# Streaming the high and low parts of the moving tokens as one operand of 512 columns in a two-block transformer kernel

## The chip, the core and the metric

The kernel runs on one core of a Trainium2 chip. The time is the device time of one execution in microseconds (us), median of several runs. TensorE (PE) does the matmuls, with a second row, PEld, for its weight loads; VectorE (DVE), ScalarE (ACT) and GpSimd (POOL) work beside it; SyncE (SP) issues most DMAs.

## The reference, cut to what matters

Two transformer blocks run on 256 tokens of width 1024, all in float32. Cut to the parts that the change touches:

```python
# block 1
x = x + merged @ w_out                                # merged: attention and pooling, gated
h2 = rmsnorm(x, norm_mlp_g)
z = square(relu(h2 @ w_up))                           # "FFN1", width 4096
x = x + z @ w_down
x = rmsnorm(x, final_norm_g)
# block 2
x = x + mix @ w_out_2                                 # mix: sparse attention and linear attention, gated
mem_n = rms_norm(mem, ln_mem_g)                       # 256 memory rows
q = rms_norm(x, ln_x_g) @ w_xq * 128 ** -0.5          # "cross attention", 4 heads of 128
k, v = split(mem_n @ w_xkv, 2)
x = x + (softmax(q @ k.T) @ v) @ w_xo
u, g = split(rms_norm(x, ln_ffn_g) @ w_up_2, 2)       # "FFN2", width 2816
u = conv_w[0] * u[t-2] + conv_w[1] * u[t-1] + conv_w[2] * u[t] + conv_b
x = x + (gelu(u) * g) @ w_down_2
return rms_norm(x, ln_final_g)
```

## The kernel before

Every large matrix product is made exact enough by splitting both sides into a high and a low part (`split`: ACT copies the high part, DVE subtracts to get the low part) and summing three matmuls: high by high, high by low and low by high (`mm3`, lines 196 to 198). Weights come in chunks of 512 KB by DMAs from SP into four `raw` buffers; ACT writes `whi` (line 158), DVE writes `wlo` (line 159), seven buffers each. Both engines run in order, so an eviction can stand behind a weight split of 1.0 to 1.2 us.

There are two forms of product. In `linB` and in the down projections (`mm_out`, `last_rows`) a block of 128 tokens is the stationary operand and 512 columns of a weight matrix move. In `linA` (and in `first_pair`, which does the same for the first two column blocks of an FFN while the tokens are still being made) a 128 x 128 piece of the weights is stationary and all 256 tokens move; the result is transposed, as the next product needs it. `linA` covers 256 output columns in two halves m = 0, 1, each of eight k steps of one `mm3`: 48 matmuls of 256 columns. Both halves lie in one PSUM bank `mm`; after both, one eviction per `linA` follows. The pools `mm` and `tp` have two banks each, `ph` four. The activations are kept as separate high and low tiles (`actah`, `actal`, `actbh`, `actbl`, and `memh`, `meml` for the memory).

FFN1 has 16 column blocks. For block b the order is `linA` of block b + 2, then 24 matmuls of 512 columns that add block b's share of the down projection into the four `ph` banks. The eviction (`relu2`) is one DVE step, max(ps, 0) times the token's scale r (the rms factor, spread over partitions as the row tile `rbc`), then the square, the copy to `zh` on ACT, and the subtraction to `zl` on DVE. FFN2 has 11 blocks; for each, two `linA` (u, then g) are followed by the 24 matmuls. Its eviction `ev_u` multiplies by the scale row, does the convolution and the gelu, and POOL multiplies by the scale row again; `ev_g` multiplies by g straight from PSUM. Cross attention uses `linA` for keys (of the memory) and queries.

`rows_bc` (lines 259 to 269) makes the scale row: POOL makes two diagonal matrices `diag` (line 265), two matmuls with a matrix of ones put them into a `tp` bank (line 266), ACT copies it out. It runs once in each FFN, between the two halves of `first_pair`, and once in the cross attention.

Each `after` step at the end of a block's last down projection transposes the new x (line 243, `tp`), multiplies by the gain and splits it. At the very end a loop over the two token blocks adds the last down projection to x (line 360), squares (ACT), multiplies by the gain (line 1356), sums (line 1359), takes the power on POOL (line 1360), scales half on ACT (line 1361) and half on DVE (line 1363), and stores each half by a DMA.

## Time and profile before

| | |
|---|---|
| runs | 832.72, 831.82, 832.34 us; median 832.34 us |
| profiled execution | 831.34 us, of which the span 829.6 us |
| TensorE busy | 809.7 us, 98% of the span |
| DVE, ACT, POOL busy | 532.9 us (64%), 441.7 us (53%), 90.5 us (11%) |
| granted TensorE clock, mean | 0.998 of full speed |
| DMA | 142 MB, mean 171 GB/s |

The span is what the profiler saw between the first and the last instruction; the execution's own time is 1.7 us longer. A row of a matmul group gives the time from a matmul's start to its modelled end, and consecutive matmuls overlap: the time that one takes from the next is read from the distance of starts, called the pitch below.

### The profile page before, as it was taken

To read this page: it belongs to the slowest core of one execution; us is meant where nothing else is said; L and a number is where in the kernel's file an instruction comes from. 1 tells how busy PE (TensorE), PEld (TensorE's weight loads), DVE (VectorE), ACT (ScalarE), POOL (GpSimd) and SP (SyncE) were. 2 spreads that over 40 slices of the span, in tenths; PEclk is the share of its full clock that TensorE was granted. 3 is DMA by queue.
4 is the path that set the end of the run, shared out by engine and by line. 5 is a ranking of instruction groups with operands and counts; after the bars stand their busy time and mean duration, and the time that the engine had idled before them with its cause. 6 is when DMAs were issued, how large, how long until landed. Compare 5 with 4: busy or idle time off the path is not lost.

```text
span 829.6 us, 12764 instructions
## 1 busy us (share of the span) xinstructions
PE 809.7 (98%) x4875; PEld 698.0 (84%) x4875; DVE 532.9 (64%) x872; ACT 441.7 (53%) x715; POOL 90.5 (11%) x144
## 2 busy tenths in 40 slices
PE   6999999999999999999999999999999999999996
PEld 5877878888999999988867778888988999999995
DVE  6757687667655555567588564579556866666563
ACT  5636565536554544556466455466554745545442
POOL 4500500102000000015000010000202100100001
PEclk9999999999999999999999999999999999999999
DMA  8854546654665565578523427672551765656621
GB/s 276 276 179 129 149 128 177 206 151 147 210 201 180 185 195 186 176 248 253 164 77 103 130 76 206 198 226 98 194 169 45 227 215 178 195 171 191 198 82 51
DMA packets 86732, 142.01 MB, mean 171 GB/s; under 512 B 5951, under 2 KB 50755, under 8 KB 86672
## 3 DMA queue, kind: packets, MB, share of 16 engines
q1 hardware_dynamic: 84976, 138.07, 54.3%
q0 software_dynamic: 1104, 1.92, 0.9%
q10 hardware_dynamic: 592, 1.22, 0.4%
q8 instruction: 38, 0.62, 0.3%
q14 instruction: 22, 0.18, 0.1%
HBM read 140.14 MB, written 1.05 MB: 170 GB/s over the span
## 4 chain that ended last, share of the span: by engine, by line
PE 90%; DVE 3%; DMA 2%; ACT 2%; POOL 1%; issue 1%; SPq 0%; POOLq 0%; ACTq 0%
PE mm L196 18%; PE mm L198 17%; PE mm L197 17%; PE ph L356 6%; PE ph L353 6%; PE ph L352 6%; PE ph L196 3%; PE ph L198 3%; PE ph L197 3%; PE tp L243 1%; DMA raw<-in_w_in 1%; DVE wlo L159 1%; PE ph L938 1%; DMA x<-in_x 1%; ACT whi L158 1%; PE ph L987 1%
## 5 line engine op out<-in xcount | busy, mean ns | idle before, releaser
L159 DVE TENSOR_TENSOR wlo<-raw,whi 128x1024 fp32r<-128x1024 f32 (+1 forms) x254 | 310.5, 1227 | 204.1 <-ACT whi L158 201.3
L158 ACT ACTIVATE whi<-raw 128x1024 fp32r<-128x1024 f32 (+1 forms) x254 | 264.9, 1051 | 229.0 <-PE mm L197 80.1
L196 PE MATMUL mm<-actbh,whi 128*128 128x256 f32 x368 | 104.1, 283 | 0.5 <-ACT actbh L158 0.5
L197 PE MATMUL mm<-actbl,whi 128*128 128x256 f32 x368 | 104.1, 283 | 0.0
L198 PE MATMUL mm<-actbh,wlo 128*128 128x256 f32 x368 | 104.1, 283 | 0.0
L353 PE MATMUL ph<-wlo,zh 128*128 128x512 f32 x188 | 73.6, 391 | 0.0
L352 PE MATMUL ph<-whi,zh 128*128 128x512 f32 x188 | 73.5, 391 | 0.0
L196 PEld LDWEIGHTS mm<-actbh,whi 128*128 128x128 f32 x368 | 69.9, 190 | 1.3 <-ACT actbh L158 1.0
L197 PEld LDWEIGHTS mm<-actbl,whi 128*128 128x128 f32 x368 | 70.0, 190 | 0.4
L198 PEld LDWEIGHTS mm<-actbh,wlo 128*128 128x128 f32 x368 | 70.0, 190 | 0.0
L196 PE MATMUL mm<-actah,whi 128*128 128x256 f32 x240 | 67.9, 284 | 0.5 <-ACT actah L158 0.5
L197 PE MATMUL mm<-actal,whi 128*128 128x256 f32 x240 | 68.0, 283 | 0.0
L198 PE MATMUL mm<-actah,wlo 128*128 128x256 f32 x240 | 67.9, 283 | 0.0
L196 PE MATMUL mm<-whi,actbh 128*128 128x512 f32 (+1 forms) x168 | 65.2, 389 | 0.1
L197 PE MATMUL mm<-wlo,actbh 128*128 128x512 f32 (+1 forms) x168 | 65.1, 388 | 0.0
L198 PE MATMUL mm<-whi,actbl 128*128 128x512 f32 (+1 forms) x168 | 64.9, 386 | 0.0
L198 PE MATMUL mm<-whi,actal 128*128 128x512 f32 x160 | 64.9, 405 | 0.0
L197 PE MATMUL mm<-wlo,actah 128*128 128x512 f32 x160 | 64.6, 404 | 0.0
L196 PE MATMUL mm<-whi,actah 128*128 128x512 f32 x160 | 64.6, 405 | 0.0
L356 PE MATMUL ph<-whi,zl 128*128 128x512 f32 x188 | 58.4, 392 | 0.0
L196 PEld LDWEIGHTS mm<-actah,whi 128*128 128x128 f32 x240 | 45.6, 190 | 1.5 <-ACT actah L158 1.0
L197 PEld LDWEIGHTS mm<-actal,whi 128*128 128x128 f32 x240 | 45.7, 190 | 0.5
(423 smaller groups left out, 1482.5 us busy)
## 6 DMA issues: line engine op xcount, KB each, us to landing
raw<-in_w_in SPq DMA_DIRECT2D x79, 512.0 KB, 4.1
raw<-in_w_up SPq DMA_DIRECT2D x76, 512.0 KB, 4.0
raw<-in_w_down SPq DMA_DIRECT2D x54, 512.0 KB, 4.3
raw<-in_w_out SPq DMA_DIRECT2D x16, 512.0 KB, 3.5
raw<-in_w_xkv SPq DMA_DIRECT2D x8, 512.0 KB, 3.9
raw<-in_w_branch_nsa SPq DMA_DIRECT2D x8, 256.0 KB, 4.3
raw<-in_w_branch_gla SPq DMA_DIRECT2D x4, 512.0 KB, 3.7
raw<-in_w_xq SPq DMA_DIRECT2D x4, 512.0 KB, 3.5
```

Of the source, the lines that this page charges most:

```text
L158: ia = A.activation(hi, src, AF.Copy)
L159: iv = sub.tensor_tensor(lo, src, hi.bitcast(F32), op=OP.subtract)
L196: PE.matmul(ps, sh, mh, start=start, stop=False)
L197: PE.matmul(ps, sh, ml, start=False, stop=False)
L198: PE.matmul(ps, sl, mh, start=False, stop=stop)
L243: PE.transpose(ps[:, j, :], src[:, (4 * b + j) * P:(4 * b + j + 1) * P], ident)
L352: PE.matmul(acc[t, n], zh, wh[:, j, sl], start=start, stop=False)
L353: PE.matmul(acc[t, n], zh, wl[:, j, sl], start=False, stop=False)
L356: PE.matmul(acc[t, n], zl, wh[:, j, sl], start=False, stop=stop)
L938: PE.matmul(banks[kvh][:, i, :], qT[rows, g0 + i, t * P:(t + 1) * P], kT_[rows, 0:W], start=True, stop=True)
L987: PE.matmul(ob[kvh * 64:(kvh + 1) * 64], kv[:, kt, v0 + kvh * 64:v0 + kvh * 64 + 64], pT[:, kt, kvh], start=br == 1 and kt == 0, stop=Fals ...
```

## The change

The high and low half of each k block of tokens lie side by side in one tile `both` of shape [128, 8, 2, 256]. For each (m, k) a new `mm_both` issues two matmuls in place of three: the high weights over 512 columns (high and low tokens at once), and the low weights over the 256 high columns. The bank then holds two partial sums of 256 columns; a new `join` copies the second one out with ACT (tile `half`) and adds the first on DVE. Half m = 0 of `linA` uses a bank of `mm`, half m = 1 a bank of `tp`, and each has its own eviction. The stationary-token products (`linB`, the down projections) stay as they are.

Around that, the evictions are rewritten. In FFN1 relu and square are done without the scale on DVE, from the joined tile; the scale, squared once on POOL, is applied to x when the down projection is added (`add_res` with r), and `rows_bc` goes. In the cross attention the queries are left unscaled and the scale enters the softmax; `rows_bc` goes there too. FFN2 keeps `rows_bc`, with its diagonals made by DVE; the first pair takes g ahead of u, POOL's product goes, and the scale for g is applied to x at the end. The final part is written out by hand as `final_rows`: its last 512 columns become two pieces of 256 in two `mm` banks, and token block 0 is stored by one DMA. The tiles `acta`, `actb` and `memT` replace the pairs of tiles, with the same bytes.

```diff
+    def mm_both(ps, sh, sl, both, start, stop):
+        if start:
+            PE.matmul(ps, sh, both, start=True, stop=False)
+        PE.matmul(ps[:, 1, :], sl, both[:, 0, :], start=False, stop=False)
+        if not start:
+            PE.matmul(ps, sh, both, start=False, stop=stop)
+    def join(dst, ps, scale=None):
+        j = junkp.tile([P, S], F32, name="half", bufs=2)
+        A.activation(j, ps[:, 1, :], AF.Copy, scale=1.0 if scale is None else scale)
+        if scale is None:
+            V.tensor_tensor(dst, ps[:, 0, :], j, op=OP.add)
+        else:
+            V.scalar_tensor_tensor(dst, ps[:, 0, :], scale, j, op0=OP.mult, op1=OP.add)
     def act_pair(slot):
-        return [acts.tile([P, 8, S], F32R, name=f"act{slot}{p}") for p in "hl"]
+        both = acts.tile([P, 8, 2, S], F32R, name=f"act{slot}")
+        return both[:, :, 0, :], both[:, :, 1, :], both
...
-            G.tensor_scalar(dg, ident, rs[t], None, op0=OP.mult)
+            V.tensor_scalar(dg, ident, rs[t], None, op0=OP.mult)
...
     def linA(hl, kts, w, ev):
-        h, l = hl
+        both = hl[2]
         per = CH // 256
         ch = [wchunk([(w[k0 * P:(k0 + per) * P, :], 0)], per, 256) for k0 in range(0, kts, per)]
-        ps = mmp.tile([P, 2, S], F32, name="mm")
         for m in range(2):
+            ps = mmp.tile([P, 2, S], F32, name="mm") if m == 0 else tpp.tile([P, 4, P], F32, name="tp").rearrange(
+                "p (a b) c -> p a (b c)", a=2)
             for k in range(kts):
                 sl = slice(m * P, (m + 1) * P)
                 wh, wl = ch[k // per]
                 j = k % per
-                mm3(ps[:, m, :], wh[:, j, sl], wl[:, j, sl], h[:, k, :], l[:, k, :], k == 0, k == kts - 1)
-        ev(ps, slice(0, 2))
+                mm_both(ps, wh[:, j, sl], wl[:, j, sl], both[:, k], k == 0, k == kts - 1)
+            ev(ps, m, True)
...
-        pss = [[(mmp, php)[i].tile([P, 512], F32, name=("mm", "ph")[i])[:, 0:S] for _ in range(2)] for i in range(2)]
+        pss = [[(mmp, php)[i].tile([P, 512], F32, name=("mm", "ph")[i]).rearrange("p (a c) -> p a c", a=2) for _ in range(2)] for i in range(2)]
         for c in range(2):
-            if c == 1:
+            if c == 1 and rows is not None:
...
-                        mm3(ps[m], wh[:, j, sl], wl[:, j, sl], h[:, k, :], l[:, k, :], k == 0, k == 7)
+                        mm_both(ps[m], wh[:, j, sl], wl[:, j, sl], both[:, k], k == 0, k == 7)
                     if c == 1:
-                        ev(ps[m][:, None, :], slice(m, m + 1))
+                        ev(ps[m], m, False)
...
-    def add_res(acc, t, n):
+    def add_res(acc, t, n, r=None):
         xa = x[:, t, n * 512:(n + 1) * 512]
-        V.tensor_tensor(xa, acc[t, n], xa, op=OP.add)
+        if r is None:
+            V.tensor_tensor(xa, acc[t, n], xa, op=OP.add)
+        else:
+            V.scalar_tensor_tensor(xa, acc[t, n], r, xa, op0=OP.mult, op1=OP.add)
...
-                    r2.append(rstd_row(x[:, t, :], f"r2_{t}"))
+                    r = rstd_row(x[:, t, :], f"r2_{t}")
+                    sq = keep(f"r2sq_{t}")
+                    G.tensor_tensor(sq, r, r, op=OP.mult)
+                    r2.append(sq)
...
         def relu2(b):
             z = {}
-            def ev(ps, ms):
-                n = ms.stop - ms.start
+            def ev(ps, m, whole):
                 if not z:
                     z["r"] = zp.tile([P, 2, S], F32, name="relu")
                     zs[b] = [zp.tile([P, 2, S], F32R, name=nm) for nm in ("zh", "zl")]
+                join(z["r"][:, m, :], ps)
+                if whole and m == 0:
+                    return
+                ms = slice(0 if whole else m, m + 1)
                 r = z["r"][:, ms]
                 zh, zl = (a[:, ms] for a in zs[b])
-                V.scalar_tensor_tensor(r, ps, 0.0, bc[0][:, None, :].to_broadcast([P, n, S]), op0=OP.max, op1=OP.mult)
-                A.activation(r, r, AF.Square)
+                V.scalar_tensor_tensor(r, r, 0.0, r, op0=OP.max, op1=OP.mult)
                 A.activation(zh, r, AF.Copy)
                 V.tensor_tensor(zl, r, zh.bitcast(F32), op=OP.subtract)
...
-        first_pair(h2, [up_w(b) for b in range(2)], [relu2(b) for b in range(2)], ends, lambda: bc.append(rows_bc(zp, r2)))
+        first_pair(h2, [up_w(b) for b in range(2)], [relu2(b) for b in range(2)], ends, None)
...
-                    last_rows(acc, rows(NB - 2, held, t) + rows(NB - 1, w, t), t, add_res, after)
+                    last_rows(acc, rows(NB - 2, held, t) + rows(NB - 1, w, t), t, lambda acc, t, n: add_res(acc, t, n, r2[t]), after)
...
         def k_part(i):
-            def ev(ps, ms):
-                A.activation(kx[:, 2 * i:2 * i + 2, :], ps, AF.Copy)
+            def ev(ps, m, whole):
+                join(kx[:, 2 * i + m, :], ps)
             linA(memT, 8, wkv[:, i * 256:(i + 1) * 256], ev)
-        bc = []
         def q_part(i):
-            def ev(ps, ms):
-                if not bc:
-                    bc.append(rows_bc(b3, r3))
-                V.scalar_tensor_tensor(qx[:, 2 * i:2 * i + 2, :], ps, 128 ** -0.5,
-                                       bc[0][:, None, :].to_broadcast([P, 2, S]), op0=OP.mult, op1=OP.mult)
+            def ev(ps, m, whole):
+                join(qx[:, 2 * i + m, :], ps, 128 ** -0.5)
             linA(hx, 8, I["w_xq_2"][0][:, i * 256:(i + 1) * 256], ev)
...
+            V.tensor_scalar(st[:, 0:2], st[:, 0:2], r3[t], None, op0=OP.mult)
             sp = b3r.tile([P, 2, S], F32, name="xsp")
             sm = small.tile([P, 8], F32, name="xsum")
             for i in range(2):
-                A.activation(sp[:, i, :], bank[:, i, :], AF.Exp, bias=st[:, i:i + 1], accum_out=sm[:, i:i + 1])
+                A.activation(sp[:, i, :], bank[:, i, :], AF.Exp, bias=st[:, i:i + 1], scale=r3[t], accum_out=sm[:, i:i + 1])
...
-            def ev_u(ps, ms):
-                n = ms.stop - ms.start
-                if not st:
+            def ev_u(ps, m, whole):
+                if "u" not in st:
                     st["u"] = zp.tile([P, 2, S], F32, name="u", bufs=2)
                     st["y"] = zp.tile([P, 2, S], F32, name="y")
+                join(st["u"][:, m, :], ps)
...
-                V.tensor_tensor(u, ps, rb, op=OP.mult)
+                V.tensor_tensor(u, u, rb, op=OP.mult)
...
-                G.tensor_tensor(y, y, rb, op=OP.mult)
-            def ev_g(ps, ms):
+                if b == 0:
+                    product(st["g"][:, ms], ms)
+            def ev_g(ps, m, whole):
+                if "g" not in st:
+                    st["g"] = zp.tile([P, 2, S], F32, name="g", bufs=2)
+                join(st["g"][:, m, :], ps)
+                if b and m == 1:
+                    product(st["g"], slice(0, 2))
+            def product(g, ms):
                 if b not in zs:
                     zs[b] = [zp.tile([P, 2, S], F32R, name=nm) for nm in ("zh2", "zl2")]
                 y = st["y"][:, ms]
                 zh, zl = (a[:, ms] for a in zs[b])
-                V.tensor_tensor(y, y, ps, op=OP.mult)
+                V.tensor_tensor(y, y, g, op=OP.mult)
...
+        def final_rows(b, w):
...
+            def square(t, sl, n, eng):
+                xa = x[:, t, sl]
+                if eng is A:
+                    jk = junkp.tile([P, D], F32, name="junk")
+                    A.activation(jk[:, sl], xa, AF.Square, scale=D ** -0.5, accum_out=sss[t][:, n:n + 1])
+                else:
+                    V.scalar_tensor_tensor(xos[t][:, sl], xa, 1.0 / D, xa, op0=OP.mult, op1=OP.mult,
+                                           accum_out=sss[t][:, n:n + 1])
...
+            for zh, zl, wh, wl in old[1]:
+                mm3(acc[1, 0], zh, zl, wh[:, 0, lo], wl[:, 0, lo], False, False)
+            piece(1, 512, D, acc[1, 1], old[1], False)
+            piece(1, 0, 512, acc[1, 0], new[1], False)
+            square(1, lo, 0, A)
+            gained(1, lo)
+            piece(1, 512, 768, tails[0], new[1], True)
+            square(1, q2, 1, A)
+            gained(1, q2)
+            V.tensor_tensor(sss[1][:, 0:1], sss[1][:, 0:1], sss[1][:, 1:2], op=OP.add)
+            piece(1, 768, D, tails[1], new[1], True)
+            square(1, q3, 2, V)
+            s0 = scale(1, 2)
+            xo = xos[1]
+            A.activation(xo[:, 0:512], xo[:, 0:512], AF.Identity, scale=s0)
+            A.dma_start(osrc[:, 1, 0:512], xo[:, 0:512])
+            V.scalar_tensor_tensor(xo[:, q3], x[:, 1, q3], s0, gfin[:, q3], op0=OP.mult, op1=OP.mult)
+            V.tensor_scalar(xo[:, q2], xo[:, q2], s0, None, op0=OP.mult)
+            SP.dma_start(osrc[:, 1, hi], xo[:, hi])
...
-        first_pair(hf, up_ws(0), gated(0), ends, lambda: bc.append(rows_bc(fp, r6)))
+        first_pair(hf, up_ws(0)[::-1], gated(0)[::-1], ends, lambda: bc.append(rows_bc(fp, r6)))
...
+                final_rows(b, w)
```

TensorE, FFN1, from the end of one block's down projection into the next `linA` (`ph` down projection, `mm` the `linA`), before:

```order
L352 MATMUL ph<-whi,zh 128x512
L353 MATMUL ph<-wlo,zh 128x512
L356 MATMUL ph<-whi,zl 128x512 x2
L196 MATMUL mm<-actah,whi 128x256
L197 MATMUL mm<-actal,whi 128x256
L198 MATMUL mm<-actah,wlo 128x256
L196 MATMUL mm<-actah,whi 128x256
L197 MATMUL mm<-actal,whi 128x256
L198 MATMUL mm<-actah,wlo 128x256
```

and in the changed kernel:

```order
L373 MATMUL ph<-whi,zh 128x512
L374 MATMUL ph<-wlo,zh 128x512
L377 MATMUL ph<-whi,zl 128x512 x2
L204 MATMUL mm<-acta,whi 128x512
L205 MATMUL mm<-acta,wlo 128x256 x2
L207 MATMUL mm<-acta,whi 128x512
L205 MATMUL mm<-acta,wlo 128x256
L207 MATMUL mm<-acta,whi 128x512
```

Three matmuls of 256 columns per (m, k) become one of 512 and one of 256; the down projection around them keeps its order.

TensorE, FFN1, between the two halves of `first_pair`, before (`tp<-diag,ones` is `rows_bc`):

```order
L196 MATMUL ph<-actah,whi 128x256
L197 MATMUL ph<-actal,whi 128x256
L198 MATMUL ph<-actah,wlo 128x256
L266 MATMUL tp<-diag,ones 128x128 x2
L196 MATMUL mm<-actah,whi 128x256
L197 MATMUL mm<-actal,whi 128x256
L198 MATMUL mm<-actah,wlo 128x256
```

and in the changed kernel:

```order
L207 MATMUL ph<-acta,whi 128x512
L205 MATMUL ph<-acta,wlo 128x256
L207 MATMUL ph<-acta,whi 128x512
L205 MATMUL mm<-acta,wlo 128x256
L207 MATMUL mm<-acta,whi 128x512
L205 MATMUL mm<-acta,wlo 128x256
```

The two matmuls of the scale row are gone from between the halves.

VectorE, the end of the program, before (`x<-ph` adds the last down projection, `xo` is the output tile, `ss` the sum of squares):

```order
L360 TENSOR_TENSOR x<-ph,x 128x512
L1359 SCALAR_TENSOR_TENSOR ss<-ss 128x1
L1356 TENSOR_TENSOR xo<-x,gain 128x512
L1363 TENSOR_SCALAR xo<-xo,ss 128x512
L360 TENSOR_TENSOR x<-ph,x 128x512
L1356 TENSOR_TENSOR xo<-x,gain 128x512
L1359 SCALAR_TENSOR_TENSOR ss<-ss 128x1
L1363 TENSOR_SCALAR xo<-xo,ss 128x512
```

and in the changed kernel:

```order
L1385 SCALAR_TENSOR_TENSOR x<-mm,r_1_5838,x 128x256
L1397 TENSOR_TENSOR xo<-x,gain 128x512
L1397 TENSOR_TENSOR xo<-x,gain 128x256
L1425 TENSOR_TENSOR ss<-ss 128x1
L1385 SCALAR_TENSOR_TENSOR x<-mm,r_1_5838,x 128x256
L1393 SCALAR_TENSOR_TENSOR xo,ss<-x 128x256
L1401 SCALAR_TENSOR_TENSOR ss<-ss 128x1
L1432 SCALAR_TENSOR_TENSOR xo<-x,ss,gain 128x256
L1433 TENSOR_SCALAR xo<-xo,ss 128x256
```

After the last matmul's piece come steps of 256 columns in place of 512, with no scaling step of token block 0 between them.

## Rows read from the trace of the kernel before

**Rows 1.** The page: the span, busy time by engine, the chain by engine.

```profile
span 829.6 us, 12764 instructions
...
PE 809.7 (98%) x4875; PEld 698.0 (84%) x4875; DVE 532.9 (64%) x872; ACT 441.7 (53%) x715; POOL 90.5 (11%) x144
...
PE 90%; DVE 3%; DMA 2%; ACT 2%; POOL 1%; issue 1%; SPq 0%; POOLq 0%; ACTq 0%
```

**Rows 2.** Groups by form: first matmul of a triple, the two largest groups. Columns: count | busy, mean | idle.

```profile
L196 PE MATMUL mm<-actbh,whi 128*128 128x256 f32 x368 | 104.1, 283 | 0.5 <-ACT actbh L158 0.5
...
L196 PE MATMUL mm<-actah,whi 128*128 128x256 f32 x240 | 67.9, 284 | 0.5 <-ACT actah L158 0.5
```

**Rows 3.** Timeline of PE: start, length, then the instruction; FFN1, then cross attention.

```profile
300.37 0.39 PE L352 MATMUL ph<-whi,zh 128*128 128x512 f32 x1
...
302.43 0.39 PE L353 MATMUL ph<-wlo,zh 128*128 128x512 f32 x1
...
304.49 0.28 PE L196 MATMUL mm<-actah,whi 128*128 128x256 f32 x1
...
306.89 0.28 PE L198 MATMUL mm<-actah,wlo 128*128 128x256 f32 x1
...
587.23 0.28 PE L196 MATMUL mm<-memh,whi 128*128 128x256 f32 x1
...
588.82 0.28 PE L198 MATMUL mm<-memh,wlo 128*128 128x256 f32 x1
```

**Rows 4.** Windows of one FFN1 block and one FFN2 block, busy time by engine.

```profile
core 0: us, PE busy (x) PEld busy (x) DVE busy (x) ACT busy (x) POOL busy (x), PEclk, DMA share, GB/s
222.70:233.94 11.24, 11.24 (x73) 10.26 (x73) 6.10 (x7) 5.50 (x7) 0.00 (x0) 1.00 0.62 188
709.82:726.83 17.01, 17.01 (x121) 16.02 (x121) 10.80 (x14) 8.51 (x11) 1.30 (x1) 1.00 0.60 186
```

**Rows 5.** Groups by form: 256-column evictions from PSUM elsewhere in the kernel.

```profile
L1252 DVE TENSOR_TENSOR actal<-ph,actah 128x256 fp32r<-128x256 f32 x4 | 1.5, 418 | 0.2 <-ACT actah L1251 0.2
...
L1251 ACT ACTIVATE actah<-ph 128x256 fp32r<-128x256 f32 x4 | 1.5, 384 | 0.9 <-PE ph L1248 0.9
```

**Rows 6.** Timeline of PE, the first pair of FFN1.

```profile
189.77 0.50 PE L196 MATMUL mm<-actah,whi 128*128 128x256 f32 x2 [0.53 <-ACT actah L158]
...
196.06 0.38 PE L266 MATMUL tp<-diag,ones 128*128 128x128 f32 x2
...
197.40 0.36 PE L196 MATMUL mm<-actah,whi 128*128 128x256 f32 x1
```

**Rows 7.** Timeline of PE and DVE, the cross attention.

```profile
586.09 0.60 PE L266 MATMUL tp<-diag,ones 128*128 128x128 f32 x4
586.45 0.37 PE L196 MATMUL mm<-memh,whi 128*128 128x256 f32 x1
...
588.15 1.23 DVE L159 TENSOR_TENSOR wlo<-raw,whi 128x1024 fp32r<-128x1024 f32 x1 [1.10 <-ACT whi L158]
...
590.03 0.70 PE L1222 MATMUL ph<-kx,qx 128*128 128x256 f32 x2 [0.93 <-DVE qx L1209]
```

**Rows 8.** Timeline of PE, the first pair of FFN2.

```profile
632.70 0.50 PE L196 MATMUL mm<-actbh,whi 128*128 128x256 f32 x2 [0.53 <-ACT actbh L158]
...
639.09 0.38 PE L266 MATMUL tp<-diag,ones 128*128 128x128 f32 x2
...
640.34 0.36 PE L196 MATMUL mm<-actbh,whi 128*128 128x256 f32 x1
```

**Rows 9.** Timeline of all engines, the end of the program.

```profile
821.55 0.40 PE L198 MATMUL ph<-whi,zl 128*128 128x512 f32 x1
...
822.48 0.49 DVE L1363 TENSOR_SCALAR xo<-xo,ss 128x512 f32<-128x512 f32 x1 [0.46 <-POOL ss L1360]
...
822.88 0.68 DVE L360 TENSOR_TENSOR x<-ph,x 128x512 f32<-128x512 f32 x1
...
825.24 0.72 ACT L1361 ACTIVATE xo<-xo,ss 128x512 f32<-128x512 f32 x1 [0.85 <-POOL ss L1360]
```

More of the change, by code (lines that the diff above doesn't have):

```diff
@@ L248, in gain_split @@
     def gain_split(p, hl, t, k):
-        h, l = (a[:, k:k + 2, t * P:(t + 1) * P] for a in hl)
+        h, l = (a[:, k:k + 2, t * P:(t + 1) * P] for a in hl[:2])
         return split(h, l, p[:, k % 4:k % 4 + 2, :])
@@ L776, in body @@
         w1t = []
[L777 to L778 removed]
+        w1b = acts.tile([P, 2, 16, P], F32, name="acta")
+        for i, nm in enumerate(("cmp_w1_k_2", "cmp_w1_v_2")):
+            w1 = w1b[:, i]
             SP.dma_start(w1, I[nm][0].rearrange("(m p) h -> p m h", p=P))
@@ L1173, in body @@
         SP.dma_start(mem, I["mem_2"][0].rearrange("(t p) d -> p t d", p=P))
-        memT = [b3.tile([P, 8, S], F32R, name=nm) for nm in ("memh", "meml")]
+        memb = b3.tile([P, 8, 2, S], F32R, name="memT")
+        memT = memb[:, :, 0, :], memb[:, :, 1, :], memb
         for t in range(NT):
@@ L1294, in gated @@
             st = {}
-            def ev_u(ps, ms):
-                n = ms.stop - ms.start
-                if not st:
+            def ev_u(ps, m, whole):
+                if "u" not in st:
                     st["u"] = zp.tile([P, 2, S], F32, name="u", bufs=2)
                     st["y"] = zp.tile([P, 2, S], F32, name="y")
+                join(st["u"][:, m, :], ps)
+                if whole and m == 0:
+                    return
+                ms = slice(0 if whole else m, m + 1)
+                n = ms.stop - ms.start
                 u, y = st["u"][:, ms], st["y"][:, ms]
                 rb = bc[0][:, None, :].to_broadcast([P, n, S])
-                V.tensor_tensor(u, ps, rb, op=OP.mult)
+                V.tensor_tensor(u, u, rb, op=OP.mult)
                 for i in range(n):
```

62 lines of the change are left out of this document (34 added, 28 removed).

## The prediction, made before the changed kernel was run

> **What bounds the kernel now.** I read the page first: TensorE is busy 809.7 of 829.6 us, and the chain of work that ended last lies on it for 90% [rows 1]. So the time falls only where TensorE gets less to do, or where it waits. Idle time is 829.6 - 809.7 = 19.9 us in all, and the 8.05 us behind the last matmul, which starts at 821.55 [rows 9], are the largest piece that the change touches. Next the groups by form: the first matmul of a triple over moving tokens is there 368 and 240 times in its two large groups and is almost never preceded by idle time [rows 2]. The whole count follows from the code: 16 column blocks of FFN1, 22 `linA` of FFN2 and 4 in the cross attention, each 2 x 8 triples, 42 x 16 = 672 triples (the first pairs count as blocks), 2016 matmuls of 256 columns.
>
> A group's mean (283 ns) is no price, since matmuls overlap. The price is the pitch, the distance of starts, read from the timeline. In a down projection of FFN1 nine steps of 512 columns take 302.43 - 300.37 = 2.06 us, 0.2289 each; in the `linA` behind it twenty steps of 256 columns take 306.89 - 304.49 = 2.40 us, 0.1200 each [rows 3]. Twice 0.1200 is 0.2400, more than 0.2289: a matmul carries some 11 ns that don't shrink with its columns. A block of FFN1 shows that nothing else is in it: 48 x 0.1200 + 24 x 0.2289 = 11.25 us against the 11.24 us of its window, TensorE busy throughout; in FFN2 96 x 0.1200 + 24 x 0.2289 = 17.01 against 17.01 [rows 4]. The other engines have slack there: DVE is busy 6.10 and 10.80 us, ACT 5.50 and 8.51 us.
>
> **The change part by part.** *The matmuls.* A triple costs 3 x 0.1200 = 0.3600 us, the new pair 0.2289 + 0.1200 = 0.3489. The saving is 0.0111 us a pair, times 672 is 7.5 us. That a 512 next to a 256 costs neither more nor less than each in its own row is borne out where `linA` meets a down projection: the period of the blocks above would not close otherwise. The unseen part is the strict alternation of the two, with a new weight piece each time. Bounds: one quiet stretch of the cross attention has 14 steps of 256 columns in 588.82 - 587.23 = 1.59 us, 0.1136 each [rows 3]; if the 256-column half of each pair went at that, the pair costs 0.3425 and the saving is 0.0175 x 672 = 11.8 us. On the other side, if the pair took as long as the triple, the saving is nothing. I take 7.5, since the row at 0.1200 is of FFN1 itself, where most of the work is.
>
> The Trainium skill, "TensorE: Matmul & The Clock Gate", section "Back-to-back issue gap", speaks against a good part of this: it puts a warm matmul at N / 2.4 ns and 2.5 ns besides, so that one matmul fewer would be worth only 2.5 ns here, an estimate of 672 x 2.5 ns = 1.7 us in place of 7.5. The trace of this kernel doesn't agree: by 2 x 120.0 - 228.9 the fixed part is 11 ns [rows 3]. What that does to the time is the first rival below.
>
> *The evictions added.* Each of 42 x 2 = 84 halves gets a join: an ACT copy of 256 columns, a DVE add of 256 columns. The nearest rows, evictions of 256 columns, have 384 ns on ACT and 418 ns on DVE [rows 5]. In an FFN1 block that is 2 of each: DVE 6.10 + 0.84 = 6.94 us (the relu step stays one step of 512 columns), ACT 5.50 + 0.77 less the square of 512 columns, some 0.7 (512 columns at the end take 0.72 [rows 9]), about 5.6. One `linA` is 16 pairs, 16 x 0.0111 = 0.18 us less, so the period falls to 11.06. In an FFN2 block it is four of each: DVE 10.80 + 1.67 = 12.5 us, ACT 8.51 + 1.54 = 10.0, of a period of 17.01 - 32 x 0.0111 = 16.65 us. Neither is full, so the cost is nothing while the weight splits stay ahead of TensorE. The cover is that slack of 4 us or more a block. Were it gone, each microsecond over the period would cost 11 us over the FFN2 blocks. The second bank per `linA` comes from `tp`, which has nothing else to do inside the FFN loops, and a bank is needed again a whole block later in FFN1 and half a block later in FFN2, 5 us or more against an eviction of about 1.
>
> *The scale row in FFN1.* The two matmuls of line 266 hold TensorE from 196.06 to 197.40, where one matmul would have been 1.34 us sooner [rows 6]. They go. At the pair's start, though, matmuls over the high tokens alone ran from 189.77 on, ahead of the subtraction that makes the low half [rows 6]; the new first matmul needs both halves, so about two of these, 0.2 us, come to stand idle. Net -1.15 us (between -1.35 and -0.9).
>
> *The cross attention.* Line 266 takes 586.45 - 586.09 = 0.36 us of TensorE, and the scores wait: the last `linA` matmul starts at 588.82 [rows 3], the first score matmul at 590.03, for `qx` on DVE, which stands behind a weight split begun at 588.15 for 1.23 us [rows 7]. That is 1.21 us for one pitch of 0.12, so 1.09 idle. With the scale in the softmax the queries' eviction needs no scale row and can be done before that split. The whole gain is 1.45 us; the added small scaling of the maxima, four times, lies in a softmax that other heads' matmuls cover only partly, and the memory's last key half now has a join of its own behind a split. I take -1.15, bounds -0.36 to -1.45, and if the join lands behind the split as `qx` did, the low end is what is left.
>
> *The scale row in FFN2* stays, with the diagonals on DVE: 639.09 to 640.34, 1.25 us, against the 0.36 us that it takes where nothing is late [rows 7, 8]. DVE is at that place with the splits of the first chunks, so it may be late too; I take the 0.89 us as won, and 0.4 lost at the start, where the matmuls at 632.70 ran ahead on the high half [rows 8]. Net -0.5, bounds -0.9 to +0.9 (a diagonal behind a split of 1.23 us [rows 7]).
>
> *The end.* The last matmul starts at 821.55; DVE's add of 512 columns begins only at 822.88, since the scaling of token block 0 stands before it from 822.48, and the last scaling begins at 825.24 [rows 9]. The span ends at 829.6, 8.05 us after that matmul. In the new order block 0's scaling is on ACT, so the add can begin some 0.4 to 0.5 us sooner, and it has 256 columns in place of 512: by the 418 ns against 680, 0.26 us less on the add and as much on the square, which now follows on DVE. Against that, the two scalings on DVE become three steps with one on ACT beside them, and the last 512 columns cost six matmuls of 256 in place of three of 512, 6 x 0.120 - 3 x 0.229 = +0.03 us. I take -0.7, bounds 0 to -1.5.
>
> *Sum* on the profiled execution: -7.5 - 1.15 - 1.15 - 0.5 - 0.7 = -11.0, so 831.34 - 11.0 = 820.3. The median of the runs is 832.34, 1.0 above this execution, so I put 821.3. The other edits (POOL's product in FFN2, 90.5 us of POOL's work in all being far from full [rows 1], and the joined tiles) cost nothing: they lie beside TensorE.
>
> **The rivals.** *The pair costs what the triple did.* For it: nothing in the trace alternates 512 and 256 over new weights throughout, and the weight load of each matmul may be what sets 0.120. Against it: the rows at 0.2289 load weights as often. Then the 7.5 us are missing: 821.3 + 7.5 = 828.8. By the page's price of a matmul, named above, it would be 821.3 + 7.5 - 1.7 = 827.1.
>
> *The evictions become the bound, and it ends slower.* The place is FFN2: DVE runs in order, and a join waits there for ACT's copy of the same bank, which may itself stand behind a weight split of ACT, so DVE stands idle in front of its own splits. TensorE then waits for `wlo`. It ends slower than before once it costs over 11 us: over 11 blocks, 1.0 us a block, that is DVE needing 16.65 + 1.0 = 17.7 us a block where the sum of its work is 12.5. Its idle waits would have to be 5.2 us a block, 1.3 for each of four joins, more than a split each time. Twice the deciding price, 2.0 us a block, gives 821.3 + 22 = 843; at 1.2 us a block it is 834.5. Against it: the windows show that DVE's waits today are filled by slack.
>
> *More is gained than counted.* If every 256-column half went at 0.1136 as in the quiet stretch [rows 3], 4.3 us more: 817.0; with the bounds of the cross attention and the end, 815.9.
>
> *The change doesn't do what it says.* The order of the changed kernel has one 512 and one 256 at each place of a triple, so this I leave out.
>
> **How the numbers follow.** The forecast, 817.5 to 824.5 around 821.3, gets 0.76; the pair at the triple's price, with or without the page's 1.7 us, 0.08; the evictions partly in the way (up to 11 us lost) 0.06, and as the bound with a slower kernel 0.04; more gained 0.06. The range 815.5 to 827.0 takes in the forecast, the larger gain and most of the partly lost cases, and leaves out under 0.2. A measurement of this kernel can tell about 0.2%, 1.7 us, from no change. Slower by more than that: 0.04; within it, where the lost matmul gain and lost cover come together: 0.04; faster: 0.92.
>
> **What would show it.** An FFN1 block's period near 11.06 us and an FFN2 block's near 16.65, TensorE still at 98% busy; starts 0.229 behind each 512 and 0.120 behind each 256; no matmul of a diagonal in FFN1 and the cross attention, and at most 0.1 us of idle time ahead of the first scores; 8.05 us from the last matmul to the end falling to about 7.3; DVE's share up to about 70%. Wrong would be idle time of TensorE released by `wlo` or by a join in the FFN loops, or a pair whose two starts are 0.36 us apart.

## The result and the profile after

The changed kernel takes 825.72 us (median of eight runs, 822.8 to 829.01) against 832.53 us for the kernel before on the same occasion, 6.8 us between the medians. The ratio is 0.9897, 95% interval 0.9869 to 0.9926: some 1% faster. The forecast was 821.3 us within 815.5 to 827.0. The profiled execution took 823.84 us, 7.5 less than the one before.

The page: span, busy time by engine, and the chain by engine.

```profile
span 822.1 us, 11535 instructions
...
PE 803.2 (98%) x4201; PEld 661.3 (80%) x4201; DVE 562.8 (68%) x965; ACT 457.1 (56%) x777; POOL 66.8 (8%) x128
...
PE 90%; DMA 3%; DVE 2%; ACT 2%; issue 1%; SPq 0%; POOLq 0%; POOL 0%; DVEq 0%; ACTq 0%
```

Beside [rows 1]: 674 matmuls fewer, 6.5 us less TensorE time, the kernel as much bound by TensorE as before. Now one block of FFN1 and one of FFN2, as in [rows 4], from the first down matmul of the block to that of the next (start and end us, length, then busy time by engine, clock, DMA):

```profile
core 0: us, PE busy (x) PEld busy (x) DVE busy (x) ACT busy (x) POOL busy (x), PEclk, DMA share, GB/s
219.26:230.34 11.08, 11.08 (x57) 9.38 (x56) 6.86 (x9) 5.53 (x7) 0.00 (x0) 1.00 0.64 209
686.51:703.19 16.68, 16.68 (x90) 14.26 (x88) 12.17 (x18) 9.70 (x15) 0.00 (x0) 1.00 0.62 190
```

DVE and ACT take on about what was worked out (6.94 and 5.6 us; 12.5 and 10.0), and TensorE doesn't stop. A piece of the `linA` in PE's timeline, which answers to [rows 3]:

```profile
302.35 0.40 PE L204 MATMUL mm<-acta,whi 128*128 128x512 f32 x1
302.59 0.39 PE L205 MATMUL mm<-acta,wlo 128*128 128x256 f32 x2
302.82 0.40 PE L207 MATMUL mm<-acta,whi 128*128 128x512 f32 x1
303.05 0.28 PE L205 MATMUL mm<-acta,wlo 128*128 128x256 f32 x1
303.17 0.39 PE L207 MATMUL mm<-acta,whi 128*128 128x512 f32 x1
...
307.95 0.39 PE L373 MATMUL ph<-whi,zh 128*128 128x512 f32 x1
```

Sixteen pairs take 307.95 - 302.35 = 5.60 us, 0.350 a pair. The sum is as predicted; its two parts aren't quite: on average over the two FFN loops the next start comes 0.234 us behind a 512 and 0.116 behind a 256, not 0.229 and 0.120.

Where the 7.5 us between the two profiled executions lie, by starts of the same instructions in both (us):

| stretch | before | after | difference | of it matmul pairs |
|---|---|---|---|---|
| first matmul to the end of block 1's projection (last transposes of x) | 187.33 | 188.38 | +1.05 | |
| to the first down matmul of FFN1 (first pair and one `linA`) | 18.44 | 16.99 | -1.45 | -0.48 |
| to the first matmul on the memory | 365.29 | 363.42 | -1.87 | -2.10 |
| to the first value product of the cross attention | 41.66 | 40.93 | -0.73 | about 0 |
| to the last transposes of x ahead of FFN2 | 17.54 | 17.34 | -0.20 | |
| to the first down matmul of FFN2 | 24.21 | 23.05 | -1.16 | -0.65 |
| to the last matmul | 163.86 | 161.35 | -2.51 | -2.91 |
| to the end | 8.05 | 7.84 | -0.21 | |

The first matmul starts 0.43 us earlier after than before, so the sum of the last column but one, -7.1, and that make the 7.5. The pairs of the two FFNs (608 at 10.1 ns) are 6.1 of it.

The 64 pairs of the cross attention together gave next to nothing. On the memory 256 columns went at 0.1136 us already before [rows 3], which is 0.341 a triple; a pair takes (594.88 - 592.76) / 6 = 0.353 there, and is the dearer one:

```profile
592.76 0.39 PE L207 MATMUL tp<-memT,whi 128*128 128x512 f32 x1
...
594.88 0.40 PE L207 MATMUL tp<-memT,whi 128*128 128x512 f32 x1
```

On the queries a pair takes 0.352 on average, a triple took 0.359. Why the memory's steps were shorter before isn't shown.

The waits of TensorE after (in total, times, longest; left out are 4.1 us for `x` from its DMA at the start, and two of 0.2):

```profile
PE mm L150 <- POOL ident L140: 2.8, 1, 2.8
PE tp L263 <- DVE x L383: 1.6, 2, 0.8
PE tp L1264 <- DVE xsp L1260: 1.1, 1, 1.1
PE mm L150 <- ACT ups L548: 0.9, 1, 0.9
```

There is no wait for `wlo`, a join or a bank in the FFN loops. The wait for `qx` of [rows 7] is gone; a new one for `xsp`, the scaled probabilities, has come.

### The profile page after: what moved, and what is told of

Its sections match the earlier page's. It is cut to its first block, busy times and chain, and to the rows that moved or that the text cites. A ratio compares the mean times of both kernels' runs of the same rounds, so it can differ in the third digit from the quotient of the medians.

```text
span 822.1 us, 11535 instructions
## 1 busy us (share of the span) xinstructions
PE 803.2 (98%) x4201; PEld 661.3 (80%) x4201; DVE 562.8 (68%) x965; ACT 457.1 (56%) x777; POOL 66.8 (8%) x128
## 3 DMA queue, kind: packets, MB, share of 16 engines
HBM read 140.14 MB, written 1.05 MB: 172 GB/s over the span
## 4 chain that ended last, share of the span: by engine, by line
PE 90%; DMA 3%; DVE 2%; ACT 2%; issue 1%; SPq 0%; POOLq 0%; POOL 0%; DVEq 0%; ACTq 0%
PE mm L196 9%; PE mm L198 9%; PE mm L197 9%; PE mm L207 8%; PE tp L207 7%; PE ph L377 6%; PE ph L373 6%; PE ph L374 6%; PE mm L205 4%; PE tp L205 4%; PE ph L198 2%; PE ph L197 2%; PE ph L196 2%; DMA raw<-in_w_in 2%; PE tp L263 1%; PE mm L204 1%
## 5 line engine op out<-in xcount | busy, mean ns | idle before, releaser
L196 PE MATMUL mm<-whi,actb 128*128 128x512 f32 (+1 forms) x168 | 65.3, 390 | 0.1
L198 PE MATMUL mm<-whi,acta 128*128 128x512 f32 x160 | 65.2, 407 | 0.0
L196 PE MATMUL mm<-whi,acta 128*128 128x512 f32 x160 | 65.1, 408 | 0.0
L197 PE MATMUL mm<-wlo,actb 128*128 128x512 f32 (+1 forms) x168 | 65.1, 387 | 0.0
L197 PE MATMUL mm<-wlo,acta 128*128 128x512 f32 x160 | 64.9, 406 | 0.0
L198 PE MATMUL mm<-whi,actb 128*128 128x512 f32 (+1 forms) x168 | 64.8, 386 | 0.0
L207 PE MATMUL mm<-actb,whi 128*128 128x512 f32 x168 | 59.7, 394 | 0.0
L207 PE MATMUL tp<-actb,whi 128*128 128x512 f32 x154 | 55.3, 398 | 0.0
L205 PE MATMUL mm<-actb,wlo 128*128 128x256 f32 x192 | 49.6, 278 | 0.0
L205 PE MATMUL tp<-actb,wlo 128*128 128x256 f32 x176 | 45.8, 281 | 0.0
L207 PE MATMUL mm<-acta,whi 128*128 128x512 f32 x112 | 39.7, 394 | 0.0
L205 PEld LDWEIGHTS mm<-actb,wlo 128*128 128x128 f32 x192 | 36.1, 188 | 2.1
```

The costliest lines, as they stand in the source:

```text
L196: PE.matmul(ps, sh, mh, start=start, stop=False)
L197: PE.matmul(ps, sh, ml, start=False, stop=False)
L198: PE.matmul(ps, sl, mh, start=False, stop=stop)
L205: PE.matmul(ps[:, 1, :], sl, both[:, 0, :], start=False, stop=False)
L207: PE.matmul(ps, sh, both, start=False, stop=stop)
```

## The experiments

**The same kernel again.**

> The changed kernel once more, nothing edited, on another occasion. Its eight runs so far lie in two groups, 822.8 to 823.8 us at a mean granted clock of 0.997 to 0.998, and 827.6 to 829.0 us at 0.992 to 0.995. Theory (the clock): the same two groups come again, near 823 and 828 us, and the lower clock goes with the longer time in each; FFN blocks keep 11.09 and 16.68 us. Rival (a wait in the program that comes out one way or the other): the times of the two groups differ at the same granted clock.

Median 824.96 us (823.51 to 829.1, seven runs; before 832.54, 830.19 to 837.7, nineteen runs; ratio 0.9916, 0.9886 to 0.9947). Five executions lie between 823.5 and 826.6, two at 829.1. The profiled one lies at 824.96 with an FFN1 block of 11.09 and an FFN2 block of 16.68 us, the same to 0.01 us; that is one of the short executions, and the traces of two longer ones further down (826.03 and 826.95) have the same blocks, so what varies is not in the FFN loops. As the theory has it, the lower clock goes with the longer time: 0.994 and 0.996 for the two at 829.1, 0.995 for 826.6, 0.997 to 0.998 for the others. Whether the clock is all of it, these times don't show.

**The pairs alone.**

```diff
-                V.scalar_tensor_tensor(r, r, 0.0, r, op0=OP.max, op1=OP.mult)
+                V.scalar_tensor_tensor(r, r, 0.0, bc[0][:, None, :].to_broadcast([P, n, S]), op0=OP.max, op1=OP.mult)
+                A.activation(r, r, AF.Square)
...
+                G.tensor_tensor(y, y, rb, op=OP.mult)
...
-                final_rows(b, w)
+                for zh, zl, wh, wl in rows(NB - 2, held, 1):
...
```

> The kernel before with the pairs alone: one 512 and one 256 for each triple, halves joined at eviction, but scale rows, relu with scale and square, POOL's product, the order of the first pair and the end of the program as before. Theory (the matmul pitch carries the gain): 672 x 0.0101 = 6.8 us less than before, about 825.5 us against 832.3, FFN blocks as in the changed kernel (11.09 and 16.68 us). Rival (the rewritten evictions and the end carry a good part): less than 4 us less than before, 828 or more.

Median 825.05 us (824.1 to 825.75, six runs), ratio 0.9901 (0.9876 to 0.9926): the theory's 825.5. The rewritten scales show in its trace by stretch: the one with the first pair of FFN1 takes 18.18 us against 16.99 in the whole change, the one of FFN2 23.77 against 23.05. `rows_bc` stands there still:

```profile
197.19 0.38 PE L286 MATMUL tp<-diag,ones 128*128 128x128 f32 x2
198.05 0.49 PE L286 MATMUL tp<-diag,ones 128*128 128x128 f32 x2 [0.48 <-POOL diag L285]
```

These 1.9 us are real in the traces, but medians of six and seven runs don't show them beside the spread told below.

**Three matmuls again.** All evictions as changed, the 512 columns in two halves wherever k is not 0.

```diff
-            PE.matmul(ps, sh, both, start=False, stop=stop)
+            PE.matmul(ps[:, 0, :], sh, both[:, 0, :], start=False, stop=False)
+            PE.matmul(ps[:, 1, :], sh, both[:, 1, :], start=False, stop=stop)
```

> The changed kernel with three matmuls of 256 columns again at every k but the first of a half: 588 of 672 pairs are triples, all evictions and the rest as changed. Theory: 588 x 0.0101 = 5.9 us more than the changed kernel, an FFN1 linA 5.594 + 14 x 0.0101 = 5.735 us, an FFN2 pair of them 11.188 + 28 x 0.0101 = 11.47. Rival (the new pair costs what a triple does, and the gain is from elsewhere): within 1 us of the changed kernel.

Median 830.47 us (827.77 to 833.37, twelve runs), ratio 0.9967 (0.9945 to 0.9989), 5.5 us over the unedited changed kernel beside it (824.96). In its trace a `linA` of FFN1 takes 5.728 us against 5.594, a pair of them in FFN2 11.474 against 11.188: 134 ns over 14 triples and 286 over 28, 9.6 and 10.2 ns each. PE's timeline shows the 256-column steps at 0.12 us:

```profile
303.59 0.28 PE L207 MATMUL mm<-acta,whi 128*128 128x256 f32 x1
303.71 0.28 PE L208 MATMUL mm<-acta,whi 128*128 128x256 f32 x1
303.83 0.28 PE L205 MATMUL mm<-acta,wlo 128*128 128x256 f32 x1
303.94 0.28 PE L207 MATMUL mm<-acta,whi 128*128 128x256 f32 x1
```

That settles the main term: the gain is the count of matmuls in the FFNs. The Trainium skill, "TensorE: Matmul & The Clock Gate", section "Back-to-back issue gap", gives a gap of N / 2.4 + 2.5 ns for a warm matmul (one at full clock) by itself, and says, which the prediction left out, that in a stream the weight loads have a part in the spacing as well; by the 2.5 ns alone the undone 588 pairs would have cost 1.5 us, an estimate. The measurement decides: about 10 ns each in the FFNs here, all at a granted clock of 1.00. In the memory's products of the cross attention the undone pairs cost nothing (0.347 us a triple on average in this run, 0.352 a pair).

**The old end.** The loop over two token blocks in place of `final_rows`, with r6 in the add.

> The changed kernel with the end of the program as it was: the loop over two token blocks, full steps of 512 columns, two DMAs each; the scale of the second FFN is applied in the add. Theory (the new end gives nothing: 18.82 us from the start of the last down projection to the end before, 18.83 after): within 0.3 us of the changed kernel. Rival (it does give the 0.7 us predicted, hidden by something else in that execution): 0.7 us more.

Median 827.92 us (822.48 to 829.4, seven runs), not apart from the changed kernel. In the trace the stretch from the last block's down projection to the end takes 824.3 - 805.07 = 19.23 us against 18.83 in the changed kernel and 18.82 before: the new end is worth 0.4 us in these executions. That the joins and the scaled add cost as much, so that nothing was left, is argued and not shown. So neither the theory (nothing) nor 0.7 is right.

This run gave more by chance. Here is PE's wait in the attention of block 1, and the granted clock in windows behind it:

```profile
49.03 0.26 PE L150 MATMUL mm<-ident,gin 48*128 48x48 f32 x1 [1.82 <-ACT ups L548]
```

```profile
51.00:52.00 1.00, 1.00 (x9) 1.00 (x9) 1.00 (x1) 0.00 (x0) 0.00 (x0) 0.72 0.66 197
52.00:53.00 1.00, 1.00 (x6) 1.00 (x6) 0.78 (x2) 0.00 (x0) 0.00 (x0) 0.50 0.87 301
53.00:54.00 1.00, 1.00 (x6) 1.00 (x5) 0.27 (x1) 0.00 (x0) 0.00 (x0) 0.50 0.71 176
```

TensorE stood still for 1.82 us, and 2.4 us after that its clock was granted at 0.50 (1.2 GHz) for about 3.4 us. The place is part of neither the diff nor the prediction.

**Filling that wait.** Eight matmuls whose results nobody reads, five of which stand right ahead of the transpose at line 150.

```diff
+        fill = opp.tile([P, 512], F32, name="o")
+        for _ in range(8):
+            PE.matmul(fill, hT[0][:, 0, 0:P], hT[2][:, 0], start=True, stop=True)
...
```

> The changed kernel with eight matmuls of 512 columns more, whose results nothing reads. By the order three stand among the first weight chunks and five right before the transpose of the gains at 48.9 us, where TensorE waits 0.6 to 1.8 us for an eviction behind a weight split; in the run with 1.82 us of wait there (old end) the granted clock fell to 0.50 from 51 to 54.7 us. Theory (the longer group of executions comes from that wait and the clock that falls behind it): five matmuls fill 1.1 us of the wait, no execution lies in the group near 828 us, all within about 822.5 to 825. Rival (the second group has another place or cause): both groups come again, 823 and 828.

Median 824.07 us (822.34 to 825.31, six runs; the kernel before beside it 835.0, 831.16 to 838.83), ratio 0.9877 (0.9847 to 0.9907). TensorE's wait there is gone from the trace, and no execution lies over 825.4. With six runs that alone could be luck (the pairs alone, with the wait left in, have none over 825.8 in six either); the last run below isn't.

**The softmax ahead of the split.** The weight splits of the second query part are issued behind the first two maxima, and behind their scaling.

```diff
-        q_part(1)
+        q_part(1, [list(maxes), list(scaled_p)])
...
```

> The changed kernel with the weight splits of the second query part issued behind the maxima of the first two softmaxes in the cross attention (first chunk) and behind their scaling (second chunk). Theory (the cross attention's gain was taken back by the wait of 1.13 us for the scaled probabilities at 590.6, since the maxima stood behind a split of 1.23 us): that wait falls to under 0.3 us, the stretch from the first scores to the value product is 0.8 to 1.1 us shorter. Rival (the next split comes late instead, TensorE waits for wlo there): the wait moves, nothing is gained.

Median 823.97 us (822.56 to 828.78, six runs), ratio 0.9881 (0.9847 to 0.9916). The timeline of DVE in the changed kernel, then in this one, shows the step that was moved:

```profile
586.10 1.23 DVE L159 TENSOR_TENSOR wlo<-raw,whi 128x1024 fp32r<-128x1024 f32 x1 [1.34 <-ACT whi L158]
587.24 1.28 DVE L1252 TENSOR_REDUCE xmax<-ph 128x2 f32<-128x512 f32 x2
```

```profile
584.73 1.29 DVE L1258 TENSOR_REDUCE xmax<-ph 128x2 f32<-128x512 f32 x2 [0.79 <-PE ph L1256]
585.94 0.42 DVE L1259 TENSOR_SCALAR xmax<-xmax,r 128x2 f32<-128x2 f32 x2
586.26 1.22 DVE L159 TENSOR_TENSOR wlo<-raw,whi 128x1024 fp32r<-128x1024 f32 x1
```

and TensorE's transposes of the probabilities, in the changed kernel and in this one:

```profile
590.60 0.70 PE L1264 MATMUL tp<-ident,xsp 128*128 128x128 f32 x4 [1.13 <-DVE xsp L1260]
```

```profile
588.10 0.70 PE L1271 MATMUL tp<-ident,xsp 128*128 128x128 f32 x4
```

The wait is gone in this execution, and the stretch from the first matmul on the memory to the first value product takes 40.16 us against 40.93: 0.77 less, just under the theory's 0.8 to 1.1. But one trace each doesn't show that size, for the stretch varies by itself: 40.37 with a wait of 0.61 in the same kernel again, 40.58 to 41.05 in four other runs here that leave this part as it was, 39.67 and no wait in the run with joins twice; with the edit 40.14 in the run with the changed end and 41.23 in the combined kernel. So the wait that was meant is gone in all three traces with the edit, but in the combined kernel one like it came further on, and what the edit is worth stays open.

**Every join twice.**

```diff
+        for _ in range(2):
             A.activation(j, ps[:, 1, :], AF.Copy, scale=1.0 if scale is None else scale)
             if scale is None:
                 V.tensor_tensor(dst, ps[:, 0, :], j, op=OP.add)
...
```

> The changed kernel with every join done twice: a second ACT copy and a second DVE add for each of 84 halves, about 0.38 and 0.42 us each, 32 us more of ACT and 35 us more of DVE. Theory (the evictions are covered): FFN blocks stay 11.09 and 16.68 us, the whole moves by under 1 us. Rival (the cover is nearly used up): FFN2 blocks grow by up to 4 x 0.42 = 1.7 us each, 15 us or more in all.

Median 823.24 us (822.41 to 826.95, six runs), ratio 0.9874 (0.9842 to 0.9905): no slower against the kernel before than the unedited changed kernel on its occasions. An FFN2 block in its trace, from the first down matmul of one block to that of the next:

```profile
672.76:689.45 16.69, 16.69 (x89) 14.25 (x88) 14.20 (x23) 11.09 (x20) 0.00 (x0) 1.00 0.65 204
```

DVE is busy 14.20 us in place of 12.17 (13.68 in the blocks behind it), the length of a block unchanged. The cover is there, with room for the joins once more. This execution (826.95) also was one of the long ones. The waits, ACT's timeline and the clock show why:

```profile
PE mm L150 <- ACT ups L549: 2.7, 1, 2.7
```

```profile
45.40 1.06 ACT L158 ACTIVATE whi<-raw 128x1024 fp32r<-128x1024 f32 x1 [1.00 <-DMA raw<-in_w_in]
48.23 1.06 ACT L158 ACTIVATE whi<-raw 128x1024 fp32r<-128x1024 f32 x1 [1.77 <-DMA raw<-in_w_in]
49.19 1.25 ACT L549 ACTIVATE ups<-mm,r 128x512 f32<-128x512 f32 x2
```

```profile
51.00:55.00 4.00, 4.00 (x21) 4.00 (x20) 2.30 (x5) 0.38 (x1) 0.00 (x0) 0.51 0.67 173
```

ACT stands in front of a weight chunk whose DMA is late, and the eviction of `ups` that TensorE needs is queued behind it. How late the DMA is differs from execution to execution. The stretch up to block 1's projection takes 192.22 us here, 188.38 in the changed kernel's profile: 3.8 us, where the whole execution is 3.1 longer. The longer wait (2.66 us in place of 0.94) is 1.7 of it.

**A changed end.** On top of the softmax edit, POOL takes the gain of the last block's first 512 columns and a sum, and DVE scales and gains a quarter in one step.

```diff
-            gained(1, lo)
+            G.tensor_tensor(xos[1][:, lo], x[:, 1, lo], gfin[:, lo], op=OP.mult)
...
-            gained(1, q2)
-            V.tensor_tensor(sss[1][:, 0:1], sss[1][:, 0:1], sss[1][:, 1:2], op=OP.add)
+            G.tensor_tensor(sss[1][:, 0:1], sss[1][:, 0:1], sss[1][:, 1:2], op=OP.add)
...
-            V.tensor_scalar(xo[:, q2], xo[:, q2], s0, None, op0=OP.mult)
+            V.scalar_tensor_tensor(xo[:, q2], x[:, 1, q2], s0, gfin[:, q2], op0=OP.mult, op1=OP.mult)
```

> The softmax edit of the run before, and a changed end: the gain of the last token block's first 512 columns and the sum of its first two squares go to POOL, the two quarters are scaled and gained in one DVE step each. Theory (the end gave nothing since DVE's last add waits 0.9 us behind gains and a sum that waits for ACT, and the last scaling is two steps in a row): the last add starts 0.3 us behind the last matmul's end, the end comes 0.4 to 0.7 us earlier on top of the softmax edit. Rival (POOL's gain of 512 columns takes 1.28 us or more and holds up the power): no gain at the end.

Median 825.01 us (821.53 to 830.93, eight runs), ratio 0.9896 (0.9862 to 0.9931); four of the eight were long ones. By the trace it does a little more than was expected: from the last matmul to the end 820.1 - 813.05 = 7.05 us against 7.84. DVE's last add and POOL's power, in the changed kernel (last matmul at 814.26) and here (813.05):

```profile
815.43 0.48 DVE L1385 SCALAR_TENSOR_TENSOR x<-mm,r,x 128x256 f32<-128x256 f32 x1
...
816.65 0.55 POOL L1402 TENSOR_TENSOR ss<-ss,neghalf 128x1 f32<-128x1 f32 x1 [5.15 <-DVE ss L1401]
...
817.64 0.34 DVE L1433 TENSOR_SCALAR xo<-xo,ss 128x256 f32<-128x256 f32 x1
```

```profile
813.36 0.48 DVE L1392 SCALAR_TENSOR_TENSOR x<-mm,r,x 128x256 f32<-128x256 f32 x1 [0.20 <-PE mm L198]
...
814.78 0.55 POOL L1409 TENSOR_TENSOR ss<-ss,neghalf 128x1 f32<-128x1 f32 x1 [0.31 <-DVE ss L1408]
```

The add starts 0.31 us behind the last matmul's start in place of 1.17, the power 1.73 in place of 2.39.

**The eviction ahead of the late chunk**, alone and with the two edits above: one weight split of ACT and DVE is issued behind the eviction of `ups`.

```diff
+            upse.append(A.activation(ups[:, t, :], ps, AF.Identity, scale=r1[t]).ins)
...
+        late[made_n[0] + 5] = upse[1:2]
...
+        g = late.pop(made_n[0], gate)
+        with behind(g):
```

> The changed kernel with that one edit alone: the eviction of ups ahead of the next weight split on ACT. Theory (a split that waits for a late weight DMA holds the eviction, TensorE waits up to 2.7 us, as in the run with joins twice, and the clock falls behind it): all executions in the group of 822 to 825 us. Rival: the group near 828 us comes again in about a third of the executions.

> The softmax edit and the changed end together with a third: in the attention of block 1 the weight split that stands on ACT ahead of the eviction of ups (and waits there for its DMA) is issued behind it. Theory (the three waits are the ones found in the traces): the transpose of the gains waits under 0.9 us in every execution, no execution in the group near 828 us; about 821 us in most, 11 to 12 us under the kernel before. Rival (the split that is put off is missed later, or the second group has another cause): executions near 826 to 828 come again.

Alone: median 822.75 us (821.36 to 823.13, five runs; before 832.76), ratio 0.9869 (0.9846 to 0.9892). Together with the softmax and the end: median 821.76 us (819.92 to 824.17, five runs), ratio 0.9865 (0.9842 to 0.9888), the fastest of all, though not apart from the former. None lies near 828. The combined kernel's profiled execution (824.17) was its longest: there TensorE waited 1.02 us for a copy of `qT` that DVE has behind another split, the clock fell to 0.50 from 51 to 54 us, and TensorE waited 1.11 us for `xsp` from 604.88 on, for the probabilities of the second pair of heads, which stood behind a split on DVE. So these edits shorten the waits in some executions, not in all. Five runs without a long one are few: the run below, of the same occasion and with that eviction where it was, has none near 828 in six either.

**A longer wait.** The last eviction of `ups` four times over.

> The changed kernel with the last eviction of ups done four times in a row on ACT (three of them over), so that TensorE's wait for it is 1.9 us or more longer in every execution. Theory (that wait, where it is 1.8 us or more, is followed by a stretch at granted clock 0.50): the clock falls behind it in the trace for 3 us or more, and the whole is 3.5 to 5.5 us longer than the changed kernel's short group of 823, 826.5 us or more in every execution. Rival (the wait alone counts): 1.9 to 3 us longer at an undisturbed clock.

Median 824.17 us (821.61 to 826.4, six runs). This missed its aim: the three repeats came to stand behind the next weight split, TensorE had other work by then, and line 150 waited 1.4 us, no longer than by chance. At 1.4 us the clock stayed at 1.00, as it did at 0.94 in the changed kernel, at 1.25 in the pairs alone and, elsewhere (at 383 us), at 1.59 in the same kernel again; it fell at 1.82 and 2.66, and in the combined kernel after 0.20 and 1.02 in a row. So it decides between neither theory: the cause that it was to make wasn't made.

**The kernel before with that one edit.**

> The kernel before with the one edit in the attention of block 1: the eviction of ups ahead of the next weight split on ACT. The kernel before has executions of 830.2 to 833.9 us and of 834.6 to 838.8 us, as the changed kernel has two groups. Theory (the second group is no work of the change but of that place, in both kernels): with the edit nearly all executions lie at 830 to 833.5 us. Rival (the groups are of another cause): executions of 835 us and more in a third of the cases again.

Median 831.19 us, and all twelve runs lie between 830.35 and 833.27; the unedited kernel before beside them has seventeen between 830.9 and 838.67, six of them over 835.5; ratio 0.9972 (0.9952 to 0.9991). The theory holds: in the kernel before the long executions come from that place in block 1, and so they are no work of the change. That the changed kernel's come from there too is seen in the run with joins twice, and fits the ten runs with the edit, none of them long. That the fall of the clock comes from the wait, and not from something that goes with it, wasn't shown by a run of its own.

## Why the prediction was right, and where it was 4 us short

The direction, the mechanism and the main size were right, and 825.72 lies in the range, near its upper end.

*The matmuls:* 0.3489 us a pair were predicted, 0.3496 measured in the FFNs (5.594 / 16), 10.1 ns saved in place of 11.1, 6.1 us for their 608 pairs. The other 64 stand in the cross attention, were priced by the pitch of FFN1 like the rest, and gave next to nothing: 6.1 us in all in place of 7.5. For half of them the rows said so: at the quiet stretch's 0.1136 [rows 3] a triple is 0.341, less than the 0.3489 of a pair. The prediction read that row the other way, as a chance of more (its bound of 11.8 us). Undoing the pairs alone gave nearly all of it back. The rival that a pair costs what a triple did is ruled out by the FFN blocks, 11.09 and 16.68 us.

*The evictions:* priced at nothing, and right; the rival in which they become the bound fell with the joins done twice.

*The scale row in FFN1:* -1.15 predicted; the stretch of the first pair lost 1.45, of which 0.48 are pairs, so -0.97, and 0.1 more lies ahead of it: a wait of 0.79 us ahead of the transposes takes the place of the earlier 0.53 and three matmuls, which now stand in the stretch itself. About -1.1 in all.

*The scale row in FFN2:* -0.5 predicted, -1.16 + 0.65 = -0.5 measured.

*The cross attention:* -1.15 predicted. The stretch lost 0.73 us in the profiled execution; with the pairs at nothing or some 0.1 dearer, that leaves -0.7 to -0.8, inside the bounds, and by the same kernel's other trace (40.37) some -1.3. The scale row and the wait for `qx` did go, 1.45 us; the step that the prediction left out was the next one on the same engine. DVE had the next weight split ahead of the maxima, and TensorE waited 1.13 us for the probabilities. Other parts of the stretch, between the scores and the products around them, got shorter; that the sum came near is in part luck.

*The end* failed: -0.7 predicted, 0.0 measured from the last down projection on (18.82 and 18.83 us). The power did come 0.72 us earlier after the last matmul (2.39 against 3.11), but the last matmul came 0.22 us later after the start of that block's down projection, and from the power to the end 5.45 us went in place of 4.94. The scalings aren't the reason: the last one ended 1.33 us behind the start of the power, against 1.30 before. The rest lies in the two last stores, of 256 KB each, issued within 0.03 us of each other: they took 2.9 and 2.7 us to land, in place of 2.1 and 2.5 before, and of 2.1 and 2.6 in the run with the changed end, which issued them 0.16 us apart. That they hinder each other is argued, not shown.

*What no step named:* the first stretch, up to block 1's projection, was 1.05 us longer in the profiled execution, although its code is the same, and half of the eight executions were some 5 us longer than the others. Some 0.65 of the 1.05 us are TensorE's start: it took 0.43 us for 512 columns until 15.5 us from the span's start, and only until 13.9 before, and 0.23 from there on; another 0.16 is the wait at line 150. The median of 825.72 stands between two groups, 822.8 to 823.8 and 827.6 to 829.0. The prediction took the one profiled execution for the kernel and added 1.0 us for the median; by the shorter group its forecast of 821.3 is 1.5 to 2.5 us short. Between the profiled executions it is 3.5 short (11.0 against 7.5): 1.4 are the pairs, 0.7 the end, 0.3 to 0.4 the cross attention, 0.6 the start up to block 1's projection, and the rest is spread over the other stretches.

## What to carry to other kernels

Where TensorE is busy throughout, the pitch by columns (from starts in the timeline, not from mean durations) prices a change in the count of matmuls to about 10%, but only in the stretch where the pitch was read: the same change gave 10 ns a pair in the FFNs and cost 12 on the memory's products. Added evictions were free here, where the windows had shown slack for them. Where a wait is taken away, follow the chain one step further: the next consumer may stand in the same queue, behind the next weight split. Before a size is read from one trace against one trace, look at how far the stretch varies in the same kernel. Before the last per cent is explained, look at whether the kernel has two times of its own; here an eviction that stands behind a split which waits for a DMA made them.

## What the runs showed of the hardware

In the FFNs, at a granted clock of 1.00, two matmuls of 256 columns took about 11 ns more than one of 512: 120 ns each against 229. On the memory's products the same 256 columns went at 114 ns, and two of them took no longer than one of 512. Idle stretches of TensorE of 1.82 us (the old end) and 2.66 us (every join twice) in otherwise dense work were followed, 2.4 and 1.2 us after they had ended, by 3.4 and 6.8 us at a granted clock of 0.50, while ones of 1.45 and 1.59 us were not. What it takes was not settled, since 0.20 and 1.02 us close together were followed by the same fall, of 3.4 us.
